# Strassen products for a quarter of the head of a matmul with RMS norm, and the second block's transpose issued ahead of the stores

## The chip, the cores and the metric

The kernel runs on one core of a Trainium2 chip. The metric is the device time of one execution in microseconds (us); lower is better. A set has four runs of the kernel under test; "before" is run beside it on the same chip. The engines are called by the names of the profile: PE (tensor engine), PEld (its weight loads), DVE (vector engine), ACT (scalar engine), POOL (which asks for most loads) and SP (which asks for stores and transposes; SPq in the profile is its queue).

## The reference, cut to what matters

```python
# a: 2048 x 2048, b: 2048 x 2048, gamma: 2048, all float32
x = a @ b
rms = sqrt(mean(x ** 2, axis=-1, keepdims=True) + eps)
out = gamma * x / rms
```

A row of the output can be scaled only when all of its 2048 columns are summed, squared and added up.

## The kernel before

The rows of A are 16 blocks of 128. Blocks 0 to 3 are the head: they are multiplied while B streams in, in pass 1 with the left half of B and in pass 2 with the right half, by plain matmuls of 128x512. Blocks 4 to 15 come in six groups of two. Each half (j = 0, 1) of a group is done by Strassen's seven products, with sums of the quarters of A and B made on DVE. A product is eight matmuls.

This is one half of a group, cut. Work on other engines hangs on hooks between the products. On ACT the traces keep the order of the program: in the kernel before, block 8's norm runs from 93.92 us and the copy that follows it in the program at 96.49 us.

```python
def group_half(g, j, hooks):
    ...
    at_hook(0)
    p2, p5 = new_bank(), new_bank()
    product(g, j, 2, p2)
    nc.scalar.copy(out=c, in_=p2)        # ACT; product 4 below adds into p2 and must wait for it
    last_squares()
    at_hook(1)
    product(g, j, 5, p5)
    nc.vector.tensor_tensor(out=t, in0=p5, in1=c, op=ALU.add)
    at_hook(2)
    p1 = new_bank()
    product(g, j, 1, p1)
    nc.vector.tensor_tensor(out=t, in0=p1, in1=t, op=ALU.subtract)
    at_hook(3)
    product(g, j, 4, p2, start=False)    # waits for the ACT copy of p2
    ...
    at_hook(4)
    product(g, j, 3, p5, start=False)
    ...
```

The blocks of A for the next group are loaded, normed (two squares on ACT, a root), scaled to float16 and transposed by a DMA, all ahead of time.

```python
def load_after(g, mb):
    wait_for(x_chunk(2 * g + 1, 1)[:, 0:1])   # a POOL copy that waits for this tile
    load_block(mb)
...                                           # hooks of the second half, j = 1
            if g + 2 < NG:
                hook(0, load_after, g, nxt + 2)
                hook(0, load_block, nxt + 3)
                hook(5, row_norm, nxt + 2)    # on ACT, ahead of the next group's copy of p2
```

For the third group (g = 2, the first one after the head) `nxt + 2` is block 8.

## Time and profile before

| | before |
|---|---|
| time, median of the first set | 224.41 us (224.22 to 224.51) |
| span of the profiled run | 222.6 us |
| PE busy | 211.1 us, 1043 matmuls |
| last wait of PE for a load | ends 24.7 us |
| first matmul of the third group starts | 69.25 us |
| last product ends | about 214.7 us |

First the engine table of the page (busy us, share of the span, instructions) and the page's chain of waits by engine.

```profile
PE 211.1 (95%) x1043; PEld 98.6 (44%) x1043; DVE 161.8 (73%) x324; ACT 129.1 (58%) x272; POOL 24.5 (11%) x49
...
PE 83%; DMA 8%; DVE 2%; POOL 2%; issue 1%; ACT 1%; DVEq 0%; ACTq 0%; POOLq 0%
```

The chain in order of time (start, length, what) tells where that 83% lies.

```profile
7.18 17.47 DMA b<-in_b_dram
24.64 0.04 issue
...
40.00 19.64 PE acc L350 x91
...
69.41 140.08 PE acc L279 x648
```

(The last line starts where the record before it ends; the first matmul of the third group itself starts at 69.25 us.) After the streamed left half of B, only PE is in the chain until 209.5 us. So, as an estimate from this chain, a matmul taken away is worth its pitch (the time from one matmul's start to the next: 7 in 1.51 us in the chain, 215.7 ns each), and anything that opens a gap in PE costs its length. Here is the timeline around the end of the third group (start, length, engine, line, operation, and in brackets the idle time before it and what ended it).

```profile
84.70 1.64 SPq L343 DMA_DIRECT2D out_dram<-x  x2
...
87.87 0.18 POOL L121 COPY pace<-x 128x1 f32<-128x1 f32 x1 [22.86 <-DVE x L525]
88.37 1.06 POOL L115 DMA_DIRECT2D a<-in_a_dram  x2 [0.32 <-issue]
...
93.92 1.06 ACT L209 ACTIVATE sq<-a 128x1024 bf16<-128x1024 f32 x1 [1.33 <-DMA a<-in_a_dram]
...
96.29 0.29 ACT L212 ACTIVATE norm<-n 128x1 f32<-128x1 f32 x1
96.49 0.57 ACT L498 COPY x<-acc 128x512 f32<-128x512 f32 x1
...
98.81 3.62 PE L279 MATMUL acc<-t_left,head_at 128*128 128x512 bf16 x16
```

Row block 2 is stored from 84.7 us. Block 8 is asked for at 88.37 us and lands at 93.84 us, ACT norms it, makes the copy of p2 by 97.06 us, and PE needs that copy at 98.81 us. The slack is 1.7 us.

### The profile page before, as it was taken

To read this page: it belongs to the slowest core of one execution; us is meant where nothing else is said; L and a number is where in the kernel's file an instruction comes from. 1 tells how busy PE (TensorE), PEld (TensorE's weight loads), DVE (VectorE), ACT (ScalarE), POOL (GpSimd) and SP (SyncE) were. 2 spreads that over 40 slices of the span, in tenths; PEclk is the share of its full clock that TensorE was granted. 3 is DMA by queue.
4 is the path that set the end of the run, shared out by engine and by line. 5 is a ranking of instruction groups with operands and counts; after the bars stand their busy time and mean duration, and the time that the engine had idled before them with its cause. 6 is when DMAs were issued, how large, how long until landed. Compare 5 with 4: busy or idle time off the path is not lost.

```text
span 222.6 us, 3026 instructions
## 1 busy us (share of the span) xinstructions
PE 211.1 (95%) x1043; PEld 98.6 (44%) x1043; DVE 161.8 (73%) x324; ACT 129.1 (58%) x272; POOL 24.5 (11%) x49
## 2 busy tenths in 40 slices
PE   7899999999999999999999999999999999999950
PEld 2445444444454444444444444444444444444430
DVE  2427557983999989978949298837994589587692
ACT  3110002807698895799646985699478954334570
POOL 7534232300000001000100002000200000000000
PEclk9999999999999999999999999999999999999997
DMA  6999999999973499818889259945994794044045
GB/s 184 223 202 209 203 208 211 212 303 259 327 280 159 188 272 292 310 72 226 276 228 400 58 174 222 366 151 143 246 368 168 97 282 189 0 188 193 0 190 188
DMA packets 36176, 47.13 MB, mean 212 GB/s; under 512 B 21952, under 2 KB 26048, under 8 KB 34496
## 3 DMA queue, kind: packets, MB, share of 16 engines
q0 software_dynamic: 9648, 23.33, 41.6%
q1 hardware_dynamic: 26080, 22.29, 33.0%
q10 hardware_dynamic: 432, 1.31, 2.0%
q8 instruction: 8, 0.13, 0.2%
q14 instruction: 8, 0.07, 0.1%
HBM read 34.60 MB, written 16.78 MB: 231 GB/s over the span
## 4 chain that ended last, share of the span: by engine, by line
PE 83%; DMA 8%; DVE 2%; POOL 2%; issue 1%; ACT 1%; DVEq 0%; ACTq 0%; POOLq 0%
PE acc L279 63%; PE acc L350 18%; DMA b<-in_b_dram 8%; POOL early L106 1%; DVE x L617 1%; POOL b L100 1%; DVE x L620 1%; PE tbank L179 1%; PE tbank L382 1%; PE tbank L165 1%; ACT sq L291 0%; DVEq L732 0%; ACT sq L682 0%; DVE x L690 0%; DVE r L322 0%
## 5 line engine op out<-in xcount | busy, mean ns | idle before, releaser
L279 PE MATMUL acc<-b,s 128*128 128x512 bf16 x376 | 83.3, 379 | 0.0
L279 PEld LDWEIGHTS <-s 128*128 128x128 f16 x472 | 46.2, 98 | 55.7 <-DVE s L244 0.2
L350 PE MATMUL acc<-b,head_at 128*128 128x512 bf16 x240 | 55.1, 379 | 0.6 <-DMA b<-in_b_dram 0.4
L291 ACT ACTIVATE sq<-x 128x512 bf16<-128x512 f32 x62 | 39.1, 631 | 10.9 <-DVE x L520 5.1
L340 DVE SCALAR_TENSOR_TENSOR x<-x,r,gamma_sb 128x1024 f32<-128x1024 f32 x28 | 34.7, 1282 | 0.8
L209 ACT ACTIVATE sq<-a 128x1024 bf16<-128x1024 f32 x24 | 25.4, 1057 | 16.8 <-DMA a<-in_a_dram 16.4
L350 PEld LDWEIGHTS <-head_at 128*128 128x128 bf16 x240 | 22.9, 98 | 26.7 <-issue 1.1
L393 ACT COPY x<-acc 128x512 f32<-128x512 f32 x11 | 5.9, 591 | 25.1 <-PE acc L350 25.1
L231 ACT ACTIVATE head_at<-a,s 128x2048 f16<-128x2048 f32 x10 | 19.9, 1990 | 0.0
L279 PEld LDWEIGHTS <-at_even 128*128 128x128 f16 x96 | 9.4, 98 | 11.5 <-issue 0.4
L279 PEld LDWEIGHTS <-head_at 128*128 128x128 f16 x96 | 9.4, 98 | 11.3
L100 POOL DMA_DIRECT2D b<-in_b_dram x15 | 10.6, 708 | 16.0 <-DMA b<-in_b_dram 13.2
L217 DVE TENSOR_SCALAR s<-norm 128x1 f32<-128x1 f32 x12 | 1.8, 150 | 14.3 <-ACT norm L212 14.2
L244 DVE TENSOR_TENSOR s<-at_even 128x1024 f16<-128x1024 f16 x15 | 9.7, 684 | 2.8 <-DMA at_even<-head_at 2.8
L291 ACT ACTIVATION_READ_ACCUMULATOR sq<-x 128x1 f32 x62 | 11.7, 188 | 0.0
L279 PE MATMUL acc<-t_left,s 128*128 128x512 bf16 x48 | 11.3, 379 | 0.0
L279 PE MATMUL acc<-early,s 128*128 128x512 bf16 x48 | 11.3, 379 | 0.0
L279 PE MATMUL acc<-early,at_even 128*128 128x512 bf16 x48 | 11.0, 379 | 0.0
L279 PE MATMUL acc<-t_left,at_even 128*128 128x512 bf16 x48 | 10.9, 379 | 0.0
L509 ACT COPY x<-acc 128x512 f32<-128x512 f32 x10 | 5.7, 575 | 8.9 <-PE acc L279 8.9
L279 PE MATMUL acc<-t_left,head_at 128*128 128x512 bf16 x48 | 10.8, 379 | 0.0
L279 PE MATMUL acc<-early,head_at 128*128 128x512 bf16 x48 | 10.8, 379 | 0.0
(86 smaller groups left out, 205.8 us busy)
## 6 DMA issues: line engine op xcount, KB each, us to landing
out_dram<-x SPq DMA_DIRECT2D x30, 512.0 KB, 3.1
a<-in_a_dram POOLq DMA_DIRECT2D x12, 1024.0 KB, 8.5
b<-in_b_dram POOLq DMA_DIRECT2D x15, 512.0 KB, 17.1
early<-in_a_dram POOLq DMA_DIRECT2D x7, 256.0 KB, 14.8
early<-in_b_dram ACTq DMA_DIRECT2D x2, 512.0 KB, 5.9
gamma_sb<-in_gamma_dram POOLq DMA_DIRECT2D x1, 1024.0 KB, 19.9
out_dram<-x SPq DMA_DIRECT2D x3, 256.0 KB, 3.5
early<-in_a_dram SPq DMA_DIRECT2D x1, 512.0 KB, 5.7
```

The costliest lines, as they stand in the source:

```text
L100: nc.gpsimd.dma_start(out=raw[j][kp], in_=b[kp * W2:(kp + 1) * W2, j * HALF:(j + 1) * HALF].rearrange("(t p) n -> p t n", p=P))
L106: nc.gpsimd.dma_start(out=ah(kp), in_=a[0:HB * P, kp * W2:(kp + 1) * W2].rearrange("(r p) k -> p r k", p=P))
L165: nc.tensor.matmul(view[:, t, r, :], ah(kp)[:, r, t * P:(t + 1) * P], identity, is_transpose=True, start=(t == 0 and r == 0), stop=(t == 1 ...
L209: nc.scalar.activation(out=junk, in_=a32[mb][:, h * HALF:(h + 1) * HALF], func=ACTF.Square, scale=2.0 ** -8, accum_out=n2[:, h:h + 1])
L231: nc.scalar.activation(out=a16[mb], in_=a32.pop(mb), func=ACTF.Copy, scale=factor.pop(mb))
L244: nc.vector.tensor_tensor(out=s_sum[s], in0=x, in1=y, op=op)
L279: nc.tensor.matmul(bank, lhsT[:, kp, :], rhs, start=(start and kp == 0), stop=(kp == KP - 1), skip_group_check=not start)
L291: nc.scalar.activation(out=sq[:, 0:CH], in_=src, func=ACTF.Square, scale=inv_sqrt_n, accum_out=msq[mb][:, c:c + 1])
L340: nc.vector.scalar_tensor_tensor(out=x, in0=x, scalar=r, in1=gamma_sb[:, h * HALF:(h + 1) * HALF], op0=ALU.mult, op1=ALU.mult)
L350: nc.tensor.matmul(bank, head_at[:, kt, r, :], head_rhs(c, kt), start=(kt == 0), stop=(kt == KT - 1))
L393: copy(out=x_chunk(*g), in_=banks[g])
L509: nc.scalar.copy(out=x21, in_=p2)
```

## The change

The intent is to save PE time in the head: the right half of rows 2 and 3 is taken through Strassen, streamed with B, so that 64 matmuls become 56. To make room, sums on DVE, loads and squares move. Besides, in the groups from the fourth on the second block's transpose is issued ahead of the stores of the finished row block. The diff, cut to its core:

```diff
+    def stream_right(kp):                       # pass 2, per B tile: 8 plain matmuls, 3 of the pair
+        order = [(g, kt) for kt in (2 * kp, 2 * kp + 1) for g in plain]
 ...
+            for m in (2, 5):
+                pair_matmul(m, kp)
+            if kp > 0:
+                pair_matmul(1, kp - 1)
 ...
+    product(PAIR, 1, 4, pair[2], start=False)   # then 3, 7, 6, with blocks 4 and 5 transposed between
 ...
     def load_after(g, mb):
-        wait_for(x_chunk(2 * g + 1, 1)[:, 0:1])
+        wait_for(x_slot[HB + r2][:, 0:1] if g == G0 else x_chunk(2 * g + 1, 1)[:, 0:1])
         load_block(mb)
 ...                                             # third group, first half
-                hook(2, finish, 1)
-                hook(3, squares2, 2)
-                hook(4, finish, 2)
+                hook(2, pair_sums)
+                hook(2, pair_ends)              # the pair's right half is complete only here
+                hook(7, square_half, r2, 1)
 ...                                             # third group, second half
+                hook(1, take_rms, r2)
+                hook(2, finish, r2, (1, 0))     # row block 2 is scaled and stored here
-                hook(0, load_after, g, nxt + 2)
-                hook(0, load_block, nxt + 3)
+                hook(2 if g == G0 else 0, load_after, g, nxt + 2)
+                hook(2 if g == G0 else 0, load_block, nxt + 3)
 ...                                             # later groups, first half
-                hook(4 if g == G0 + 1 else 3, finish, 2 * g - 2)
+                if g > G0 + 1:
+                    hook(3, scale, 2 * g - 2)
                 hook(4, apply, nxt + 1)         # scales and transposes the second block
+                if g == G0 + 1:
+                    hook(4, scale, 2 * g - 2)
+                hook(4, store, 2 * g - 2)
```

## The prediction

> **What bounds the kernel now.** The tensor engine. The chain of waits shows one piece of DMA (the left half of B, ending at 24.64 us) and then nothing but tensor work to 209.5 us: 63% of the span on the product line, 18% on the head's matmul line. A 13 us tail follows. In that stretch a 512-column matmul costs its pitch, not its 379 ns record: the chain has 7 in 1.51 us, 215.7 ns each. [...] Granted clock is 1.00 through the body.
>
> **What the change removes.** The order of instructions shows 16 fewer entries on the tensor queue, that is 8 weight loads and 8 matmuls: four 128x512 chunks of rows 2 and 3 took 64 matmuls and take 56 as seven products. Worth 8 x 215.7 ns = 1.73 us, all on the chain.
>
> **What it adds and moves.**
> - DVE gets five sums of A for the pair (0.60 us pitch each) and four tile additions, against separate B sums it loses (16 x 0.35 us). In pass 1 DVE was busy 2.9 to 3.8 of each 5 us, so those should fit.
> - Pass 2 shrinks from about 14 matmuls per B tile to 11, 2.37 us. B tiles land every 2.5 us (spacing of the landings of 1 MB loads). The reordered queue lands the last tile at about 56.1 us; the tensor engine wants it at about 56.2. I expect 0 to 0.5 us of waiting.
> - The transposes of blocks 4 and 5 now follow pass 2 between products 7 and 6. Following each queue with durations of the trace, the scaled block 4 is ready at about 63.3 us, when product 7 reaches it; the sums for the next group come at 67.0, 69.3, 69.9 against needs at 67.5, 69.2, 71.0. Next narrow place: two more row norms on ACT (1.25 us each half) and the pair's last additions on DVE end about 81.3 us, when the bank is wanted. I give these 0 to 0.7 us together.
> - The later transposes issued ahead of the stores land about 2 us earlier (before: second transpose issued at 108.4 behind stores, DVE waits 2.8 us for it, tensor weights wait 0.2 us). That wait was off the chain, so this gains nothing itself; it keeps the earlier tensor stream from stalling there. The 1.28 us ACT table load moved to the start was in idle ACT time: no gain.
>
> **Sum.** 224.38 - 1.73 + about 0.4 of new waits = 223.0 us, range 222.5 to 224.0. Faster by over 2%: 0.02; within 2%: 0.95; slower by over 2%: 0.03.
>
> **What would show it right.** 8 fewer product/head matmuls; pass 2 ending near 59 us; first product of the third group at 67.5 to 68.2 us (before 69.4); from there the same 140.1 us of unbroken tensor work; the same tail of 13 us. **Wrong:** tensor idle before the B tiles in 40 to 57 us above 1 us; idle before weight loads of the sums at 67 to 92 us above 1 us; a changed pitch or tail.
>
> **What would make it wrong.** Slower landing of A blocks 6 and 7 (now requested about 6 us later) delaying ACT norms and, through DVE, the banks at 76 to 90 us: plus 1 to 3 us. The other way, a tail or pass 1 that I took as unchanged getting shorter.

## The result, and the profile after

| | before | after |
|---|---|---|
| time, median of four runs | 224.41 us (224.22 to 224.51) | 227.72 us (227.48 to 228.48) |
| ratio | | 1.0155 (1.0138 to 1.0173) |
| span of the profiled run | 222.6 us | 226.7 us |
| first matmul of the third group starts | 69.25 us | 67.94 us |

The ratio is the mean time of one kernel's fast runs over that of the other's of the same rounds, so it is not quite the ratio of the medians. The changed kernel is 1.5% slower. The profiled run was its slowest (228.48 us). The unedited kernel in a later set gave 227.49 us, and a third set whose edit had no effect (e8 below) 226.60 us: its executions scatter over 2 us, those of the kernel before over 0.7 us.

The same two places of the page:

```profile
PE 212.3 (94%) x1035; PEld 98.1 (43%) x1035; DVE 168.3 (74%) x330; ACT 127.1 (56%) x263; POOL 26.6 (12%) x55
...
DMA 34%; PE 30%; issue 15%; ACT 10%; DVE 7%; POOL 1%; DVEq 0%; POOLq 0%; ACTq 0%
```

Eight matmuls are gone, as meant. But PE is down from 83% to 30% of the chain, and loads and ACT are in it. (The share itself says little: up to 89 us the chain runs back through POOL's queue, with a piece of 20.89 us called issue, while PE was busy all along.) The third group started earlier, as meant; the first line is from the kernel before, the second from the changed one:

```profile
69.25 3.62 PE L279 MATMUL acc<-b,s 128*128 128x512 bf16 x16
67.94 3.73 PE L289 MATMUL acc<-b,s 128*128 128x512 bf16 x16
```

The chain in order of time shows the turn at the end of the third group:

```profile
89.17 7.48 DMA a<-in_a_dram
...
96.74 1.16 ACT sq L223 x2
...
99.30 0.57 ACT x L578
...
99.92 12.22 PE acc L289 x48
```

The timeline at the place shown of before:

```profile
86.71 2.48 DVE L366 SCALAR_TENSOR_TENSOR x<-x,r,gamma_sb 128x1024 f32<-128x1024 f32 x2
...
88.02 1.53 SPq L372 DMA_DIRECT2D out_dram<-x  x2
88.06 1.17 POOL L126 COPY pace<-x 128x1 f32<-128x1 f32 x1 [20.91 <-DVE x L366]
89.17 1.05 POOL L120 DMA_DIRECT2D a<-in_a_dram  x2
...
96.74 1.06 ACT L223 ACTIVATE sq<-a 128x1024 bf16<-128x1024 f32 x1 [6.43 <-DMA a<-in_a_dram]
...
99.30 0.56 ACT L578 COPY x<-acc 128x512 f32<-128x512 f32 x1
...
99.92 5.30 PE L289 MATMUL acc<-t_left,head_at 128*128 128x512 bf16 x16 [2.35 <-ACT x L578]
```

Read from the bottom: PE stood idle for 2.35 us for ACT's copy of p2. The copy came late because ACT, where the norm stands ahead of the copy, had stood idle 6.43 us for block 8 and then normed it (e5 below puts the copy first, and it comes at 93.87 us). Block 8 landed at 96.65 us, 2.8 us later than before. Of that, 0.8 us is a later request (89.17 against 88.37 us) and 2.0 us a slower landing (7.48 against 5.47 us). PE meanwhile came 1.4 us earlier. The slack of 1.7 us was gone, and more.

The later request has a part that is easy to miss. The POOL copy that paces the load took 1.17 us here, beside the two scalings on DVE (86.71 to 89.19 us), and 0.18 us in the kernel before. In all eight profiles of the changed kernel and its variants in which it waited for these scalings it took 1.10 to 1.18 us. No run took the scalings away, so that they are the cause is not shown.

The 16 matmuls behind the gap took 5.30 us, where the same 16 took 3.62 us before. The stretches of that time, one us each, tell why (columns: stretch, its length, PE busy and its instructions, granted clock as a share of full speed, DMA share, GB/s):

```profile
98.00:99.00 1.00, 0.00 (x0) 1.00 0.20 82
99.00:100.00 1.00, 0.09 (x1) 1.00 0.02 8
100.00:101.00 1.00, 1.00 (x4) 0.73 0.00 0
101.00:102.00 1.00, 1.00 (x4) 0.50 0.00 0
...
103.00:104.00 1.00, 1.00 (x4) 0.56 0.00 0
104.00:105.00 1.00, 1.00 (x6) 1.00 0.68 136
```

From 100 us on PE counts as busy for the whole of each us, yet only 4 matmul records fall in one, against 6 at 104 us, where the granted clock is back at 1.00: between, it was at half. The clock's record has it at half for 3.41 us from 100.46 us on. That cost 5.30 - 3.62 = 1.68 us in this run. The idle time before it was 2.35 us.

The clock's records of all twelve profiles show a pattern, which no run was made to test. Each stretch between two changes of the clock is a whole number of 3.413 us (28 of them from the first rise to the fall at 100.46 us here; 63 in the kernel before, up to its end). So, for the count, each trace is cut into windows of 3.413 us from the first rise. In the window that ended at 100.46 us PE was idle for 2.35 us, and the clock fell; in e12's it was idle for 3.30 us, and the clock fell; in e8's, at 96.04 to 99.46 us, for 1.75 us, and it did not. By the count over the twelve profiles, tails included, the clock fell after every window with 2.03 us idle or more and after none with 1.75 us or less. In e2 the clock did not fall: its 1.93 us idle were split over two windows, 1.18 us in one. That a gap of about 2 us does harm or not according to where it falls is an estimate from these counts.

From the start of the third group to the last full-width matmuls, the profiled run lost about 5.4 us: 2.5 us in the gap (by the distance of starts, less one pitch), 1.7 us by the clock, and 1.3 us in three places at 152, 175 and 177 us, where PE waited for ACT's copy again or for the DVE addition after it. The pair had won 1.3 us by 67.9 us (1.73 us for eight matmuls, less the waits of 0.25 and 0.13 us for B tiles at 47 and 56 us). That makes the 4.1 us by which the span grew.

### The profile page after: what moved, and what is told of

Read it like the earlier page. It is cut to its first block, busy times and chain, and to the rows that moved or that the text cites. A ratio compares the mean times of both kernels' runs of the same rounds, so it can differ in the third digit from the quotient of the medians.

```text
span 226.7 us, 3014 instructions
## 1 busy us (share of the span) xinstructions
PE 212.3 (94%) x1035; PEld 98.1 (43%) x1035; DVE 168.3 (74%) x330; ACT 127.1 (56%) x263; POOL 26.6 (12%) x55
## 3 DMA queue, kind: packets, MB, share of 16 engines
q10 hardware_dynamic: 432, 1.31, 1.9%
## 4 chain that ended last, share of the span: by engine, by line
DMA 34%; PE 30%; issue 15%; ACT 10%; DVE 7%; POOL 1%; DVEq 0%; POOLq 0%; ACTq 0%
PE acc L289 25%; DMA b<-in_b_dram 20%; DMA a<-in_a_dram 14%; ACT sq L223 6%; PE acc L384 4%; ACT sq L307 2%; DVE x L366 1%; DVE x L705 1%; ACT x L578 1%; DVE x L708 1%; DVE x L605 1%; DVE x L596 1%; DVE x L591 1%; DVE x L586 1%; ACT at_even L196 0%
## 5 line engine op out<-in xcount | busy, mean ns | idle before, releaser
L289 PE MATMUL acc<-b,s 128*128 128x512 bf16 x408 | 92.1, 379 | 0.0
L289 PEld LDWEIGHTS <-s 128*128 128x128 f16 (+1 forms) x512 | 49.9, 98 | 60.0 <-DVE s L264 0.4
L384 PE MATMUL acc<-b,head_at 128*128 128x512 bf16 x176 | 41.8, 379 | 0.7 <-DMA b<-in_b_dram 0.5
L307 ACT ACTIVATE sq<-x 128x512 bf16<-128x512 f32 x54 | 34.0, 630 | 11.0 <-DVE x L600 5.6
L384 PEld LDWEIGHTS <-head_at 128*128 128x128 bf16 x176 | 16.8, 98 | 20.4 <-issue 1.6
L289 PEld LDWEIGHTS <-head_at 128*128 128x128 f16 (+1 forms) x112 | 11.4, 102 | 17.4 <-issue 5.5
L426 ACT COPY x<-acc 128x512 f32<-128x512 f32 x6 | 3.4, 586 | 25.2 <-PE acc L384 25.2
L289 PE MATMUL acc<-early,head_at 128*128 128x512 bf16 x64 | 14.5, 379 | 0.0
L289 PE MATMUL acc<-early,s 128*128 128x512 bf16 x56 | 14.4, 379 | 0.0
L264 DVE TENSOR_TENSOR s<-head_at 128x1024 f16<-128x1024 f16 (+5 forms) x22 | 13.4, 636 | 0.1
L280 DVE TENSOR_TENSOR b<-b 128x1024 bf16<-128x1024 bf16 x16 | 10.8, 687 | 0.2
L289 PE MATMUL acc<-early,at_even 128*128 128x512 bf16 x48 | 10.8, 379 | 0.0
```

The source lines that it names most:

```text
L264: nc.vector.tensor_tensor(out=sum_of(g, s)[:, lo:hi, :], in0=x[:, lo:hi, :], in1=y[:, lo:hi, :], op=op)
L280: nc.vector.tensor_tensor(out=flat[:, 1:3, :], in0=flat[:, 1:3, :], in1=flat[:, 0::3, :], op=ALU.add)
L289: nc.tensor.matmul(bank, lhsT[:, kp, :], rhs, start=(start and kp == 0), stop=(kp == KP - 1), skip_group_check=not start)
L307: nc.scalar.activation(out=sq[:, 0:CH], in_=src, func=ACTF.Square, scale=inv_sqrt_n, accum_out=msq[mb][:, c:c + 1])
L384: nc.tensor.matmul(bank, head_at[:, kt, r, :], head_rhs(c, kt), start=(kt == 0), stop=(kt == KT - 1))
L426: copy(out=x_chunk(*g), in_=banks[g])
```

## The experiments

Theory A: block 8 lands late, and because its norm stands ahead of the copy in ACT's queue, PE stops; the rest follows from that. Rival B: the new order of transposes and stores is what costs. Rival C: the pair's extra work on DVE and ACT is too much. "Lead" below is the time from the landing of the first A block of a pair to PE's start of product 4 (first half of the next group), worked out from the trace. A gap is given in the text as the distance of two starts less one pitch; the idle time in a line's brackets is about 0.17 us shorter. In the profiles of the experiments some 20 matmul records are missing, one each about 10.8 us; these single missing records are not counted as gaps.

### e1: ask for blocks 8 and 9 as early as before

```diff
-        wait_for(x_slot[HB + r2][:, 0:1] if g == G0 else x_chunk(2 * g + 1, 1)[:, 0:1])
+        wait_for(x_chunk(2 * g + 1, 1)[:, 0:1])
...
-                hook(2 if g == G0 else 0, load_after, g, nxt + 2)
-                hook(2 if g == G0 else 0, load_block, nxt + 3)
+                hook(0, load_after, g, nxt + 2)
+                hook(0, load_block, nxt + 3)
```

> The changed kernel, but block 8's load is asked for as early as in the kernel before (after the first half of the third group, not after the scaling of row block 2). Theory A (block 8 lands late, and the scalar engine waits for it ahead of the copy that the tensor engine needs): the load goes out at about 86 us instead of 89.2, lands at 92 to 94 instead of 96.7, the 2.35 us tensor gap at 97.6 us and the slow-clock stretch behind it vanish, and the time falls from 227.7 to 223.2-224.2 us. Rival B (the new order of transposes and stores is what costs): the gap may go, but the later groups lose what the first one won, and the time stays above 226. Rival C (the pair's extra vector and scalar work keeps the scalar engine late): the copy stays late and the gap stays over 1.5 us.

Measured: 225.75 us (224.98 to 227.49), ratio 1.0046 (1.0023 to 1.0069): between theory A's 223.2 to 224.2 us and rival B's 226 us. The profiled run was the slowest of the four. Block 8 was asked for at 85.56 us and landed at 90.86 us, so ACT had its norm by 93.6 us. The gap shrank but did not go. The timeline shows that the copy now waited for something else:

```profile
85.56 1.05 POOL L120 DMA_DIRECT2D a<-in_a_dram  x2 [0.34 <-ACT sq L307]
...
87.58 1.53 SPq L372 DMA_DIRECT2D out_dram<-x  x2
...
97.56 0.58 ACT L578 COPY x<-acc 128x512 f32<-128x512 f32 x1 [3.96 <-DMA out_dram<-x]
...
98.20 1.89 PE L289 MATMUL acc<-t_left,head_at 128*128 128x512 bf16 x8 [1.07 <-ACT x L578]
```

The copy writes into the buffer of row block 2's right half, which is still being stored. That store was issued at 87.58 us and landed at 97.46 us, 9.9 us later, against 2.7 us for the same store in the changed kernel, where it went out ahead of the loads. Here two 1 MB loads had been issued before it. The trace of the kernel before has the same: its six stores that were issued 1.1 to 2.6 us behind the first of two such loads (asked for at 110.44, 135.39 and 158.82 us) landed after 8.3 to 11.2 us, its other stores from 70 us on after 2.5 to 4.0 us. So Theory A was incomplete: behind the late load stood a late store. In the later groups gaps came back too (at 123, 125, 149, 151, 174 and 176 us, 3.3 us in sum).

### e2: only the Strassen part, the stores back in front of the second transpose

```diff
-                if g > G0 + 1:
-                    hook(3, scale, 2 * g - 2)
+                hook(4 if g == G0 + 1 else 3, finish, 2 * g - 2)
                 hook(4, apply, nxt + 1)
-                if g == G0 + 1:
-                    hook(4, scale, 2 * g - 2)
-                hook(4, store, 2 * g - 2)
```

> The changed kernel with the stores put back in front of the second transpose, so only the Strassen part is left. Theory A: the gap at 97.6 us is there before any moved store, so it stays at about 2.3 us with its clock dip; only the small gaps of 0.25 to 0.3 us at 152, 175 and 177 us may go, and the time is 226.7 to 227.7. Rival B: the time falls to 224 or less.

Measured: 225.95 us (225.65 to 225.99), ratio 1.0064 (1.0049 to 1.0079): between the two expectations, below the 226.7 to 227.7 us of theory A and above the 224 us of rival B. The gap at 97 us stayed (2.1 us), without a clock dip:

```profile
99.23 1.89 PE L289 MATMUL acc<-t_left,head_at 128*128 128x512 bf16 x8 [1.93 <-ACT x L578]
```

The later gaps at 150 to 177 us went. One new gap came, the one that the new order was made to prevent:

```profile
118.56 1.90 DVE L264 TENSOR_TENSOR s<-at_even 128x1024 f16<-128x1024 f16 x3 [2.92 <-DMA at_even<-head_at]
...
119.31 1.90 PE L289 MATMUL acc<-b,s 128*128 128x512 bf16 x8 [0.47 <-DVE s L264]
```

The sums for the fifth group waited for the second transpose. All four runs are faster than all twelve of the changed kernel (226.34 to 228.48 us, with e8 and e13). So the order of transposes and stores is part of the loss, and it also does what it was meant to do.

### e4: fill the gap with matmuls that nobody needs

```diff
         at_hook(3)
+        if (g, j) == (G0 + 1, 0):
+            filler = ps_t.tile([P, CH], FP32, name="tbank")
+            for _ in range(9):
+                nc.tensor.matmul(filler, s_sum[1][:, 0, :], sums[0][:, 0, 0, :],
+                                 start=True, stop=True)
         product(g, j, 4, p2, start=False)
```

> The changed kernel with nine idle-time matmuls of 512 columns into an unused bank just before the product that waits at 97.6 us: they fill about 1.9 us of the 2.35 us gap with work nobody needs. If the gap itself is all that costs, nothing changes (227.7). If the halved clock behind the gap costs too (16 matmuls took 5.3 us instead of 3.6 in the profiled run), the granted clock stays 1.00 there, the 16 matmuls take 3.6 us, and the time falls by 0.5 to 1.7 us, to 226.0-227.2: runs differ in whether the dip happens.

Measured: 227.23 us (226.41 to 228.42), ratio 1.0128 (1.0092 to 1.0163). The nine matmuls ran in the gap and product 4 started at 98.86 us, with the clock at 1.00. But the profiles of e2, e8 and e13, with gaps of 1.85 to 2.1 us and no filler, have no dip either, and the time is not lower than that of e8. The run is inconclusive about the clock. What the dip costs is known only from the profiles that had one: the changed kernel's first (gap 2.5 us) and e12's (gap 3.6 us).

### e8: row block 2's stores later

```diff
-                hook(2, finish, r2, (1, 0))
+                hook(2, scale, r2, (1, 0))
+                hook(5, store, r2, (1, 0))
```

> The changed kernel with the two stores of row block 2 (512 KB each, issued at 88.0 and 89.2 us, right at block 8's load) moved three products later; the load is asked for at the same time. If these stores are why the load took 7.5 us instead of the 5.5 us of the kernel before, it lands in 5.5 to 6 us, at about 95, the gap shrinks from 2.35 to 0.5-1 us, there is no clock dip, and the time is 224.0 to 225.5. If the collision does not matter, the landing stays at 96.7 and the time at 227.7.

Measured: 226.60 us (226.34 to 227.44), ratio 1.0102 (1.0079 to 1.0125). The edit had no effect: the stores are issued by SP, whose queue has no other instruction between the two places, so the store still goes out as soon as DVE has scaled the rows (87.52 and 88.72 us in the trace; 88.02 and 89.22 us in the changed kernel's). Here moving the line in the program moved nothing. The run tells nothing about the stores and serves as a repeat of the changed kernel. The question that it asked, whether these stores slow block 8's landing, has only an indirect answer (under "What stays open").

### e5: block 8's norm behind the copy on ACT

```diff
-                hook(0, row_factor, nxt)
-                hook(1, apply, nxt)
+                if g == G0 + 1:
+                    hook(1, row_norm, nxt)
+                    hook(2, row_factor, nxt)
+                    hook(2, apply, nxt)
+                else:
+                    hook(0, row_factor, nxt)
+                    hook(1, apply, nxt)
...
-                hook(1, row_norm, nxt + 1)
+                hook(2 if g == G0 + 1 else 1, row_norm, nxt + 1)
...
-                hook(5, row_norm, nxt + 2)
+                if g > G0:
+                    hook(5, row_norm, nxt + 2)
```

> The changed kernel with its loads and stores as they are, but on the scalar engine the row norm of block 8 stands behind the copy that the tensor engine needs, not ahead of it. If the scalar queue's order is what turns the late load into a tensor gap, the copy runs at about 97 us, the gap of 2.1 to 2.5 us before it goes (under 0.5 us left there), although block 8 still lands at 95.6 to 96.7; some of it may come back as waits further on, because block 8's scaling is no earlier. Time 224.5 to 226.2 us against 226.6 of the effect-free repeat (e8). If the gap has another cause (the bank, the stores of row block 2), it stays over 1.5 us.

Measured: 226.62 us (225.41 to 227.03), ratio 1.0093 (1.0063 to 1.0124). The gap went as expected, the time did not fall to the expected 224.5 to 226.2 us.

```profile
93.87 0.58 ACT L578 COPY x<-acc 128x512 f32<-128x512 f32 x1 [3.84 <-PE acc L289]
...
96.21 1.06 ACT L223 ACTIVATE sq<-a 128x1024 bf16<-128x1024 f32 x1 [0.38 <-DMA a<-in_a_dram]
...
97.12 3.62 PE L289 MATMUL acc<-t_left,head_at 128*128 128x512 bf16 x16
```

Block 8 was as late as ever (96.13 us), but the copy stood ahead of its norm and PE did not stop. So the order of ACT's queue is what turned a late load into a gap. With the norm ahead of it (the changed kernel) the copy came at 99.30 us, behind a block that landed at 96.65 us; ahead of the norm it came at 93.87 us. The time, however, hardly fell: gaps of 1.4 and 0.5 us opened at 123 and 125 us, and smaller ones at 111, 149, 173 and 175 us. The lateness was handed on, not cured.

### e6: the kernel before with the new order of transposes and stores

The edit splits `finish` into `scale` and `store` and orders them as the change does; nothing else.

> The kernel before with only the second part of the change: the second transpose is issued ahead of the stores of the finished row block. If this order costs by itself (four stores around the next A loads in place of two), the A loads of blocks 12 to 15 land 1 to 2.5 us later after their issue than in the kernel before (which has 6.6, 10.0, 6.0 and 9.4 us), small tensor gaps show at about 147 to 172 us, and the time is 224.6 to 225.6. If it only helps, as I had predicted, the time is 224.2 to 224.5 without gaps.

Measured: 225.02 us (224.60 to 225.05), ratio 1.0025 (1.0008 to 1.0042), within the range expected if the order costs. Blocks 12 and 14 landed 8.40 and 7.58 us after their request, where the kernel before has 6.61 and 5.98 us, and gaps of 0.40 and 0.25 us opened at 149 and 173 us. The new order by itself is a small loss here. That it comes through the landing of the A loads is argued from these landings.

### e9: block 8 early, block 9 behind row block 2

As e1, but only block 8 goes out early:

```diff
-                hook(2 if g == G0 else 0, load_after, g, nxt + 2)
+                hook(0, load_after, g, nxt + 2)
+                if g == G0:
+                    hook(2, wait_for, x_slot[HB + r2][:, 0:1])
                 hook(2 if g == G0 else 0, load_block, nxt + 3)
```

> As e1, where block 8's load goes out at 85.6 us, but block 9's load waits until row block 2 is scaled, so its stores are not queued behind a second 1 MB load. In e1 the remaining gap of 1.24 us waited for a store that took 9.9 us. If that is right, the store lands within 5 us, the copy runs before 97.3 us and the gap at 97 us is under 0.3 us. The later gaps of e1 (about 3 us in sum) stay, since the stores still come behind both transposes: 224.3 to 225.3 us. If the first gap stays over 1 us, the store is not its cause.

Measured: 222.68 us (222.45 to 222.80), ratio 0.9925 (0.9911 to 0.9940). Faster than the kernel before by 1.64 us in the median, and 3.9 to 5.0 us faster than the changed kernel (226.60 us in e8, 227.49 in e13, 227.72 in the first set).

```profile
85.81 0.53 POOL L120 DMA_DIRECT2D a<-in_a_dram  x1 [0.34 <-ACT sq L307]
...
88.98 0.53 POOL L120 DMA_DIRECT2D a<-in_a_dram  x1
...
91.33 1.06 ACT L223 ACTIVATE sq<-a 128x1024 bf16<-128x1024 f32 x1 [1.22 <-DMA a<-in_a_dram]
...
93.96 0.59 ACT L578 COPY x<-acc 128x512 f32<-128x512 f32 x1
...
97.21 3.62 PE L289 MATMUL acc<-t_left,head_at 128*128 128x512 bf16 x16
```

Two loads instead of one double request, 3.2 us apart: block 8 landed in 5.44 us, the store of the buffer did not hold up the copy, and the copy was done 2.7 us before PE needed it. PE has no gap over 0.1 us from 25 us to its end (missing records aside), and its share of the page's chain is back:

```profile
PE 82%; DMA 8%; POOL 3%; DVE 2%; issue 1%; ACT 1%; DVEq 0%; ACTq 0%; POOLq 0%
```

The expected time was too high: I had thought that e1's later gaps would stay, for the stores still come behind both transposes. They went too. So in the changed kernel those gaps needed both: the late start and the new order. And e9 keeps all of the pair's extra work on DVE and ACT, so this work by itself is not the cause: rival C is out.

### e10: e9, and the old order of stores from the fifth group on

```diff
                 if g > G0 + 1:
-                    hook(3, scale, 2 * g - 2)
+                    hook(3, finish, 2 * g - 2)
                 hook(4, apply, nxt + 1)
                 if g == G0 + 1:
-                    hook(4, scale, 2 * g - 2)
-                hook(4, store, 2 * g - 2)
+                    hook(4, finish, 2 * g - 2)
```

The text below says "from the fourth group on" and "only the third group keeps the new order"; by the counting of this document, where the third group is g = 2, the old order is back from the fifth group on and the fourth keeps the new one.

> As e9, and from the fourth group on the stores stand ahead of the second transpose again as in the kernel before; only the third group keeps the new order. If late loads (first gap) and the new order (later gaps) are together the whole loss, the tensor stream has no gap over 0.5 us after 68 us, keeps the 1.5 us that the first part won, and the time is 222.8 to 223.4 us, faster than the kernel before. If something else costs, it stays above 224.

Measured: 222.64 us (222.49 to 222.78), ratio 0.9925 (0.9910 to 0.9940), the same as e9 and a little below the expected 222.8 to 223.4 us. With no late start, the order of stores does not matter: the loads of blocks 12 and 14 still land about 1 us sooner than in e9 (6.4 and 6.5 us against 7.5 us), but there is slack for both.

### e12: the kernel before, with block 8 late

```diff
-        wait_for(x_chunk(2 * g + 1, 1)[:, 0:1])
+        wait_for(x_chunk(2 * g + 1, 3 if g == G0 else 1)[:, 0:1])
...
-                hook(0, load_after, g, nxt + 2)
-                hook(0, load_block, nxt + 3)
+                hook(3 if g == G0 else 0, load_after, g, nxt + 2)
+                hook(3 if g == G0 else 0, load_block, nxt + 3)
```

> The kernel before, nothing of the change in it, with the loads of blocks 8 and 9 asked for later: after the product at 91 us instead of at 87.9. If a late block 8 is enough by itself to cause the loss, whatever the Strassen part does: the load goes out at about 92.2 and lands at 97.5-98, the copy on the scalar engine ends at about 101, a tensor gap of 2 to 2.5 us opens at 98.8, and smaller gaps follow in later groups; time 226.3 to 228.3 us, like the changed kernel. If the loss needs the pair's extra work, the gap stays under 1 us and the time under 225.5.

Measured: 229.44 us (229.10 to 229.67), ratio 1.0223 (1.0208 to 1.0238), above the expected 226.3 to 228.3 us. The load went out at 94.07 us, later than I had meant (the pacing copy took 2.38 us from 91.75 us on), so the gap was larger than expected.

```profile
94.07 1.05 POOL L115 DMA_DIRECT2D a<-in_a_dram  x2
...
101.82 0.56 ACT L498 COPY x<-acc 128x512 f32<-128x512 f32 x1
...
102.44 3.07 PE L279 MATMUL acc<-t_left,head_at 128*128 128x512 bf16 x7 [3.46 <-ACT x L498]
```

A late block 8 opens the gap in a kernel that has no Strassen pair and the old order; rival C is not needed for it. The profiled run had the clock dip as well. And no later gaps followed, against what I had expected: with the old order the lateness died out.

### e13: the changed kernel again

> The changed kernel again, unedited, beside the others on one chip, since it scattered more (227.5 to 228.5 in its first runs, 226.3 to 227.4 in the repeat whose edit had no effect) than the kernel before (224.2 to 224.9). It should give 226.3 to 228.5 us, and the runs with the lower granted clock should be the slower ones if the halved clock behind the gap comes in only some executions.

Measured: 227.49 us (226.78 to 228.30), ratio 1.0150 (1.0129 to 1.0170). The profiled run (226.78 us) had a gap of 1.85 us at 97 us, later gaps of 2.1 us in sum, and no dip. The run with the lowest mean clock (0.979) took 227.44 us and was not the slowest; the slowest had 0.988. So the scatter of the changed kernel is not settled by the clock alone. Its later gaps differ from run to run as well.

### What the runs say together

Request, landing and lead for the four pairs of A loads behind the third group, from the traces. A lead of 3.26 us is what ACT needs from landing to copy and PE's start; where the lead is 3.26 us, PE was waiting.

| run | block 8: asked for, landed | leads of blocks 8, 10, 12, 14 (us) |
|---|---|---|
| before | 88.37, 93.84 | 4.97, 4.12, 5.16, 6.53 |
| e12, before, block 8 late | 94.07, 99.17 | 3.26, 4.20, 5.33, 6.64 |
| e6, before, new order | 88.36, 93.84 | 4.97, 4.06, 3.32, 3.47 |
| changed kernel | 89.17, 96.65 | 3.26, 3.77, 3.30, 3.26 |
| e13, the same again | 88.60, 95.41 | 3.26, 3.26, 3.59, 3.26 |
| e1, loads early | 85.56, 90.86 | 7.34, 3.27, 3.26, 3.26 |
| e2, old order | 88.91, 95.97 | 3.26, 3.64, 4.91, 5.90 |
| e9, split loads | 85.81, 91.25 | 5.96, 5.65, 5.82, 6.03 |

In e1 the first gap came from the store and not from block 8, hence the long first lead. The table separates two things. The first gap needs a late block 8, or a late buffer. The later gaps need a late start and the new order together: e12 and e2 have the late start alone and recover, e9 has the new order alone and loses nothing, the changed kernel, e13 and e1 have both and come back to 3.26 us. One run does not fit so neatly: in the kernel before the new order alone (e6) brought the leads of blocks 12 and 14 down to 3.32 and 3.47 us, with two small gaps. Block 10 was asked for at 11.6 us there and at 10.8 us in e9, on the scale that follows. How the lateness is handed on can be read from the requests: block 10 was asked for 13.3 us after PE's start of product 4 in the changed kernel, e13, e1, e2 and e12, and 10.8 us after it in e9 (before: 11.6). That request waits for a DVE addition, and DVE in these runs stood waiting for norms. The view of waits has it (who waited for whom: us in total, times, longest), first for before:

```profile
DVE s L217 <- ACT norm L212: 14.2, 4, 3.9
```

and for the changed kernel:

```profile
DVE s L231 <- ACT norm L226: 24.1, 10, 4.0
PE acc L289 <- ACT x L578: 2.6, 2, 2.4
```

In e9 it is back at 14.4 us:

```profile
DVE s L231 <- ACT norm L226: 14.4, 8, 3.9
```

The total alone proves little: e6 has 21.0 us there, with block 10 asked for in time. That DVE's waits for the norms are what delays the next request is argued from these lines; no run took that one wait away.

## Why the prediction was wrong, point by point

- **Right:** what bounds the kernel, and the worth of the saving. Eight matmuls fewer; the third group began at 67.94 us, inside 67.5 to 68.2 us and 1.31 us ahead of the kernel before. With the obstacle removed, e9 is 1.64 us faster than before, where 1.73 us had been predicted for the eight matmuls. The pitch of 215.7 ns held (the 32 matmuls from 88.77 us on took 7.07 us, the last one's record of 379 ns included: 215.8 ns each).
- **Right:** the waits for B tiles (predicted 0 to 0.5 us; 0.25 and 0.13 us at 47 and 56 us) and those of the third group (predicted 0 to 0.7 us; 0.1 us).
- **Wrong, the step that failed:** "from there the same 140.1 us of unbroken tensor work". In the profiled run it took 145.6 us from the first matmul's start (before: 140.2 us): a gap of 2.5 us, 1.7 us at half clock behind it, and 1.3 us in later gaps. The sum "224.38 - 1.73 + about 0.4 of new waits" lacked this term. What failed is an overlap that was taken as given: that block 8's load and norm would stay hidden behind PE's work.
- **Why it was missed:** the prediction followed the queues up to the third group's banks and took the rest as unchanged. The slack at the next place was 1.7 us, and readable: copy done at 97.06 us, needed at 98.81 us. PE coming 1.4 us earlier spent most of it; the rest went, and 2.5 us more, with a load asked for 0.8 us later and landing 2.0 us slower. The prediction did name "slower landing of A blocks" as what could make it wrong, but blocks 6 and 7; it was block 8.
- **Wrong about the reordering:** "so this gains nothing itself; it keeps the earlier tensor stream from stalling there". The second half holds: without it, e2 has a gap of about 0.6 us at 119 us. But the order has a price that the prediction gave as zero: in the kernel before it costs 0.7 us (225.02 against 224.32 us), and behind a late start it keeps the stream late, which is 1.3 us of gaps in the first profile of the changed kernel and 2.1 us in e13's.
- **Not predicted:** the halved clock. It turned a gap of 2.5 us into a loss of 4.2 us in the run that had it.

What stays open: how much of block 8's slower landing is due to row block 2's stores, and why the changed kernel's executions scatter by 2 us. On the stores, e8 did not move them, but the landings of the other runs point their way. In the six profiles in which the load was issued 1.15 us behind the first of these stores (changed kernel, e2, e4, e5, e8, e13) it took 6.8 to 7.5 us; in the six in which it went out ahead of them (e1, e9, e10) or within 1.4 us of the last one's landing or later (before, e6, e12) it took 5.1 to 5.5 us.

## What to carry to other kernels

When a change makes the bound engine arrive earlier, list the places further on where it meets another queue, and compare the slack there with the time won. Here the slack was 1.7 us and PE came 1.4 us earlier; with block 8 landing 2.8 us later, behind which the copy had to stand in ACT's queue, that became a gap of 2.5 us. A load whose norm stands ahead of an eviction in the same queue is such a place: ask for it early (e9), and do not issue a second large load ahead of a store whose buffer is needed next (in e1 that store landed after 9.9 us, in the changed kernel after 2.7 us). Here moving one request by about 3 us was worth 3.9 to 5.0 us.
